# Moving the weight-block additions of a fast-multiplication kernel from VectorE to GpSimd

## The chip, the cores and the metric

One Trainium2 chip, one of its cores. The metric is device time in microseconds (us) of one launch of the whole kernel; the profile is one execution recorded by the hardware profiler. Engines are named as in the profile: PE is TensorE (PEld its weight loads), DVE is VectorE, ACT is ScalarE, POOL is GpSimd, SP is the engine whose queue issues most transfers.

## The reference

One transformer-like block over 528 tokens (16 learned ones ahead of 512) with 1024 features. All big steps are matrix products with large weights:

```
xn = rms_norm(h);  z = xn @ w_in              # 1024 x 10752, cut into 8 parts
o_a = rg_lru(conv(u_rnn)) * gelu(u_gate)      # recurrent branch
o_b = head_rms(retention(q, k, v)) * silu(g_ret)   # 4 heads, decayed attention
mixed = sigmoid(ga) * (o_a @ w_branch_rnn) + sigmoid(gb) * (o_b @ w_branch_ret)
h = h + mixed @ w_out
gate, val = split(conv3(rms_norm(h) @ w_up))  # 1024 x 6144
h = h + (gelu(gate) * val) @ w_down           # 3072 x 1024
out = rms_norm(h)[16:]
```

Inputs and weights are float32.

## The kernel before

Every float32 weight is used as a pair of float16 halves: a high half (scaled by 256 and rounded, a copy on ACT, L92) and a low half (the rest, one SCALAR_TENSOR_TENSOR on DVE, L93, which reads the float32 weight `raw` and the high half `wt`). The helper `split` issues both. A product of two such pairs takes three matmuls (high-high, high-low, low-high).

The weights are cut into *units* of 128 x 2048 numbers. A unit is loaded by SP into one of two `raw` buffers, and split into `wt` tiles of 1024 columns, from a ring of ten. A plain unit fills two `wt` tiles. A *fast* unit is multiplied by a seven-product scheme (Strassen's, in a form that shares sums) in place of eight block products, and fills four tiles: its quarters B11, B21 and B22 as they are, and four sums of quarters, T1 to T4. The steps of a fast unit are

1. `cut(top, left)`: split B11 (512 columns);
2. `cut(low, both)`: split B21 and B22 (1024 columns);
3. `sums`: form T1 to T4 in place in `raw`;
4. two late cuts: `cut(top, both)` splits T1 and T3, `cut(low, both)` splits T4 and T2 (1024 columns each).

There are 39 fast units: 8 for the gate of the retention branch, 4 and 4 for the two mixing gates, 8 for the retention branch's weights, 4 in the up projection and 11 in the down projection. `tick` and `get` emit their steps between the products of earlier units, as far ahead as `ahead[0]` tiles allow. PE, ACT and DVE run in an order written by hand in the first part only; after it a scheduler sets the order, and every engine then takes its instructions strictly in that order. ACT also copies partial products out of PSUM (`kept` and `last`, L872), which PE must have before it reuses the accumulator `pa`; these copies stand in the same queue as the cuts. In the early stages DVE also forms the gates (`g`, L889 to L900) in its one queue with the low halves.

The stages that hold fast units, by their place in the span: value projections and retention with its gates (220 to 400 us), the mixing of the two branches (400 to 650), the output projection without fast units (650 to 714), the up projection (714 to 948) and the down projection (948 to 1050).

Of the kernel before, what the change touches and what calls it, by code (L numbers as in the profile page):

```python
# [12 lines left out]
ALU = mybir.AluOpType  # L13
# [38 lines left out]
def hybrid_block_kernel(ctx, tc, x, meta, norm_mix_g, w_in, conv_w, conv_b, rg_a_w, rg_a_b,  # L52
                        rg_x_w, rg_x_b, lam, w_brnn, w_bret, w_out, norm_ffn_g, w_up,
                        fconv_w, fconv_b, w_down, norm_final_g, rope_t, decay_t, out):
    nc = tc.nc
# [35 lines left out]
    def split(hi, lo, src, s):  # L91
        a = nc.scalar.activation(hi, src, AF.Copy, scale=s)  # L92
        b = nc.vector.scalar_tensor_tensor(lo, src, s, hi, op0=ALU.mult, op1=ALU.subtract)  # L93
        return a.ins, b.ins
# [83 lines left out]
    for ps_ in range(2):  # L178
        for q in range(6):
            rows = w_down[4 * q * P:(4 * q + 4) * P].rearrange("(i j p) c -> p j i c", i=2, j=2)  # L180
# [56 lines left out]
    def fast_steps(rv, bk, bc):  # L237


        tiles = []  # L240
        top, low = slice(0, bk), slice(bk, 2 * bk)
        left, right = slice(0, bc), slice(bc, 2 * bc)

        def cut(rows, cols):
            def run():
                t = wsp.tile([P, 2, 1024], F16, name="wt")
                src = rv[:, rows, cols]
                n = bk * src.shape[2]
                tv = [t[:, a, :n].rearrange("p (k c) -> p k c", k=bk) for a in range(2)]
                tiles.append(tv)  # L250
                split(tv[0], tv[1], src, SW)
            return run

        def sums():
            pair = rv[:, top].rearrange("p k (h c) -> p h k c", h=2)
            nc.vector.tensor_tensor(pair, pair, rv[:, :, right].rearrange("p (h k) c -> p h k c", h=2), op=ALU.add)  # L256
            nc.vector.tensor_tensor(rv[:, low, right], rv[:, top, left], rv[:, low, right], op=ALU.add)
            nc.vector.tensor_tensor(rv[:, low, left], rv[:, low, left], rv[:, low, right], op=ALU.add)  # L258

        at = {"B11": (0, 0), "B21": (1, 0), "B22": (1, bc), "T1": (2, 0), "T3": (2, bc), "T4": (3, 0), "T2": (3, bc)}  # L260

        def form(nm, a, k):
            i, c0 = at[nm]
            return tiles[i][a][:, k, c0:c0 + bc]

        def late(run):
            def behind():
                with behind_copy():
                    run()
            behind.late = True  # L270
            return behind

        wviews.append(form)
        return [cut(top, left), cut(low, slice(0, 2 * bc)), sums,
                late(cut(top, slice(0, 2 * bc))), late(cut(low, slice(0, 2 * bc)))]

# [4 lines left out]
    def behind_copy():  # L281

        return tc.issue_after(last_keep[0]) if gating[0] and last_keep[0] else nullcontext()
# [1392 lines left out]
```

## Time and profile before

| | before |
|---|---|
| time, median of 3 runs | 1069.89 us (1067.33 to 1071.05) |
| span of the profiled execution | 1066.5 us |
| PE busy | 1048.0 us (98%) |
| DVE busy | 853.2 us (80%) |
| ACT busy | 587.9 us (55%) |
| POOL busy | 6.9 us (1%), 20 instructions |

The time of the profiled execution itself is not listed apart; its span is 3.4 us under the median of the three runs. In the views below a group's row gives engine, operation, names, shape, count, then busy time, mean duration of one, and the idle time of the engine just before them with its releaser. In the timeline a row gives start, duration, engine, line and operation, and in brackets the idle time before it. In a table by stretch the columns are stretch, its length, and busy time and count of each engine.

### The profile page before, as it was taken

Reading aid. Unit: us, or ns where it says so; the run is one execution under the profiler, and the core shown is the slowest. Engines: PE = TensorE matmul, PEld = TensorE weight load, DVE = VectorE, ACT = ScalarE, POOL = GpSimd, SP = SyncE. Lnnn points to the kernel's source line nnn. Section 1 sums busy time; section 2 is a strip of 40 time slices with the busy share of each in tenths; the row PEclk is TensorE's granted clock in tenths of the full one; section 3 lists DMA queues with packets and bytes.
Section 4 is the critical chain, followed back from the end, with each engine's and each line's share of the span. In section 5 each row is a group of like instructions: output and inputs, shape, how many; then the busy total and the mean of one; then the engine's idle time right before and its main releaser. Section 6 shows DMA issues by size and latency. Waiting matters only on the chain.

```text
span 1066.5 us, 20995 instructions
## 1 busy us (share of the span) xinstructions
PE 1048.0 (98%) x8995; PEld 851.1 (80%) x8995; DVE 853.2 (80%) x1301; ACT 587.9 (55%) x927; POOL 6.9 (1%) x20
## 2 busy tenths in 40 slices
PE   8999999999999999999999999999999999999997
PEld 6888888865685858887888885588888888888884
DVE  6884799998577878877797776479989897988965
ACT  8568954434364747655554454366566465454442
POOL 2000000000000000000000000000000000000000
PEclk9999999999999999999999999999999999999999
DMA  8341243431022312334433365032432324214322
GB/s 255 104 133 42 80 139 119 160 120 40 2 85 75 120 40 65 119 100 119 129 105 119 115 202 179 1 119 80 159 111 88 119 81 133 67 60 138 101 81 79
DMA packets 108989, 111.49 MB, mean 105 GB/s; under 512 B 5610, under 2 KB 100560, under 8 KB 108896
## 3 DMA queue, kind: packets, MB, share of 16 engines
q1 hardware_dynamic: 108448, 109.74, 32.0%
q8 instruction: 70, 1.15, 0.4%
q10 hardware_dynamic: 160, 0.27, 0.1%
q0 software_dynamic: 288, 0.14, 0.1%
q14 instruction: 23, 0.19, 0.1%
HBM read 108.04 MB, written 2.10 MB: 103 GB/s over the span
## 4 chain that ended last, share of the span: by engine, by line
PE 76%; DVE 13%; ACT 6%; DMA 2%; issue 2%; ACTq 0%; DVEq 0%
PE ps L418 31%; PE P L1512 9%; PE pa L867 7%; PE ps L930 6%; PE ps L1235 4%; DVE wt L93 4%; PE pe L867 3%; PE ps L431 3%; PE pm L418 2%; PE ps L953 2%; PE pa L1399 2%; ACT wt L92 2%; PE pb L867 2%; DVE rnn L665 1%; PE pe L1399 1%
## 5 line engine op out<-in xcount | busy, mean ns | idle before, releaser
L418 PEld LDWEIGHTS <-wt 128*128 128x128 f16 x3840 | 373.2, 97 | 58.2 <-DVE t L759 1.4
L93 DVE SCALAR_TENSOR_TENSOR wt<-raw,wt 128x1024 f16<-128x1024 f32 (+2 forms) x278 | 303.0, 1105 | 58.6 <-ACT wt L92 57.9
L92 ACT ACTIVATE wt<-raw 128x1024 f16<-128x1024 f32 (+2 forms) x278 | 261.4, 962 | 155.7 <-DVE raw L258 30.0
L867 PEld LDWEIGHTS <-wt 128*128 128x128 f16 x2016 | 195.0, 97 | 38.0 <-issue 11.2
L418 PE MATMUL ps<-x2h,wt 128*128 128x258 f16 x1184 | 181.2, 273 | 0.0
L418 PE MATMUL ps<-xh,wt 128*128 128x257 f16 (+2 forms) x1056 | 163.8, 275 | 1.1 <-DVE t L759 1.1
L418 PE MATMUL ps<-x2l,wt 128*128 128x258 f16 x592 | 113.2, 272 | 0.0
L418 PE MATMUL ps<-xl,wt 128*128 128x257 f16 (+2 forms) x528 | 102.2, 275 | 0.0
L1512 PE MATMUL P<-wt,act 128*128 128x256 f16 x792 | 88.3, 273 | 0.0
L1512 PEld LDWEIGHTS <-act 128*128 128x128 f16 x792 | 77.5, 98 | 9.0
L1377 DVE SCALAR_TENSOR_TENSOR cv<-ps,vt,cv 128x512 f32<-128x512 f32 x80 | 59.8, 748 | 22.7 <-ACT cv L1375 21.8
L867 PE MATMUL pa<-xs,wt 128*128 128x257 f16 x576 | 71.6, 273 | 5.1 <-ACT kept L872 4.7
L930 PE MATMUL ps<-wt,xh 128*128 128x512 f16 x256 | 76.1, 379 | 0.4 <-DVE v L93 0.4
L418 PE MATMUL pm<-oa,wt 128*128 128x257 f16 x480 | 55.3, 274 | 0.0
L1375 ACT ACTIVATE cv<-ps,vt,vt 128x512 f32<-128x512 f32 x40 | 30.9, 773 | 34.5 <-PE ps L418 33.8
L930 PE MATMUL ps<-wt,xl 128*128 128x512 f16 x128 | 48.5, 379 | 0.0
L930 PEld LDWEIGHTS <-xh 128*128 128x128 f16 x256 | 24.8, 98 | 29.3 <-issue 0.7
L256 DVE TENSOR_TENSOR raw<-raw 128x1024 f32<-128x1024 f32 x39 | 47.5, 1219 | 0.6
L867 PE MATMUL pa<-ob,wt 128*128 128x257 f16 x384 | 45.7, 274 | 2.0 <-ACT kept L872 1.4
L1235 PE MATMUL ps<-wt,mx 128*128 128x512 f16 x192 | 44.3, 378 | 0.0
L1399 PEld LDWEIGHTS <-wt 128*128 128x128 f16 x336 | 32.6, 97 | 4.4
L1235 PEld LDWEIGHTS <-mx 128*128 128x128 f16 x192 | 17.7, 98 | 18.4
(293 smaller groups left out, 1409.0 us busy)
## 6 DMA issues: line engine op xcount, KB each, us to landing
raw<-in_w_in SPq DMA_DIRECT2D x40, 1024.0 KB, 4.9
raw<-in_w_up SPq DMA_DIRECT2D x24, 1024.0 KB, 5.2
raw<-in_w_down SPq DMA_DIRECT2D x48, 256.0 KB, 3.5
raw<-in_w_branch_ret SPq DMA_DIRECT2D x16, 512.0 KB, 4.7
raw<-in_w_branch_rnn SPq DMA_DIRECT2D x8, 640.0 KB, 4.6
raw<-in_w_out SPq DMA_DIRECT2D x4, 1024.0 KB, 6.2
xin<-in_x SPq DMA_DIRECT2D x4, 512.0 KB, 5.6
raw<-in_w_in SPq DMA_DIRECT2D x4, 512.0 KB, 8.1
```

The costliest lines, as they stand in the source:

```text
L92: a = nc.scalar.activation(hi, src, AF.Copy, scale=s)
L93: b = nc.vector.scalar_tensor_tensor(lo, src, s, hi, op0=ALU.mult, op1=ALU.subtract)
L256: nc.vector.tensor_tensor(pair, pair, rv[:, :, right].rearrange("p (h k) c -> p h k c", h=2), op=ALU.add)
L418: nc.tensor.matmul(ps[:, hf, :n], w(aw, k, col, P), src(ax, k, c0, n), start=k == 0 and (aw, ax) == (0, 0), stop=k == nk - 1 and aw == 1)
L431: mm = nc.tensor.matmul(ps[:, hf, :n], w(aw, k, col, P), src(ax, k, c0, n), start=k == 0 and (aw, ax) == (0, 0), stop=k == KD - 1 and aw == 1)
L867: nc.tensor.matmul(ps[:, :257], ws[k // 4](wf, aw, k % 4), src(xf_, ax, k), start=first and k == 0 and (aw, ax) == (0, 0), stop=k == last_ ...
L930: nc.tensor.matmul(pb, xf(ax, k, XF + j0, nb), w(aw, k % 4, 0, 512), start=i == 0, stop=i == 23)
L1235: nc.tensor.matmul(ps[:, n], mx[k][:, a, c0:c0 + P], wo[k // 2](aw, k % 2, n * 512, 512), start=k == 0 and (a, aw) == (0, 0), stop=k == ks ...
L1375: nc.scalar.activation(vv_, src[:, :, 2:258], AF.Identity, scale=vt2[:, 96 + ch:97 + ch], bias=bias)
L1377: nc.vector.scalar_tensor_tensor(vv_, src[:, :, j:j + 256], vt2[:, 48 * j + ch:48 * j + ch + 1], vv_, op0=ALU.mult, op1=ALU.add)
L1399: nc.tensor.matmul(ps[:, :258], w(wf, aw, k), x2_form(xf_, ax, k), start=first and k == 0 and (aw, ax) == (0, 0), stop=k == 3 and aw == 1, ...
L1512: nc.tensor.matmul(pd[:, 256 * tt:256 * tt + 256], t[:, ax, c0 + tt * P:c0 + tt * P + P], w(wf, aw, i), start=q % 6 == 0 and tt == 0 and i ...
```

## The change

The three DVE additions of `sums` (one of 1024 columns, two of 512) become four additions of 512 columns, issued by GpSimd. The numbers formed are the same. The change is one line longer, so lines below it shift by one: L257 to L259 are the GpSimd additions, L873 is the copy of `kept`.

```
         def sums():
-            pair = rv[:, top].rearrange("p k (h c) -> p h k c", h=2)
-            nc.vector.tensor_tensor(pair, pair, rv[:, :, right].rearrange("p (h k) c -> p h k c", h=2), op=ALU.add)
-            nc.vector.tensor_tensor(rv[:, low, right], rv[:, top, left], rv[:, low, right], op=ALU.add)
-            nc.vector.tensor_tensor(rv[:, low, left], rv[:, low, left], rv[:, low, right], op=ALU.add)
+            for a, rows, cols, b in ((top, top, left, right), (top, low, right, right)):
+                dst = rv[:, a, cols]
+                nc.gpsimd.tensor_tensor(dst, dst, rv[:, rows, b], op=ALU.add)
+            nc.gpsimd.tensor_tensor(rv[:, low, right], rv[:, top, left], rv[:, low, right], op=ALU.add)
+            nc.gpsimd.tensor_tensor(rv[:, low, left], rv[:, low, left], rv[:, low, right], op=ALU.add)
```

The scheduler also puts other instructions in a new order. First place: the queue of DVE in the mixing stage, at the head norm of the last head (`tr`, `rt`, `rc`; about 440 us in the trace). `raw_5367` is the fast unit's weight tile there, `or3` the head's output. Before:

```order
L93 SCALAR_TENSOR_TENSOR wt_5451<-raw_5367,wt_5451 128x512
L976 RECIPROCAL rc_5350<-tr_5348 128x16
L256 TENSOR_TENSOR raw_5367<-raw_5367 128x2x4x128
L978 STREAM_TRANSPOSE rt_5346<-rc_5350 128x512
L93 SCALAR_TENSOR_TENSOR wt_5454<-raw_5367,wt_5454 128x1024
L1043 TENSOR_TENSOR or3_4793<-or3_4793,rt_5346 128x514
L1043 TENSOR_TENSOR or3_4794<-or3_4794,rt_5346 128x514
L257 TENSOR_TENSOR raw_5367<-raw_5367 128x4x128
L93 SCALAR_TENSOR_TENSOR wt_5492<-raw_5367,wt_5492 128x1024
L258 TENSOR_TENSOR raw_5367<-raw_5367 128x4x128
L1043 TENSOR_TENSOR or3_4795<-or3_4795,rt_5346 128x514
```

The same place after the change, where the tile is `raw_5375`:

```order
L93 SCALAR_TENSOR_TENSOR wt_5459<-raw_5375,wt_5459 128x512
L975 STREAM_TRANSPOSE tr_5356<-rt_5354 128x512
L978 RECIPROCAL rt_5354<-rt_5354 128x2
L977 RECIPROCAL rc_5358<-tr_5356 128x16
L93 SCALAR_TENSOR_TENSOR wt_5462<-raw_5375,wt_5462 128x1024
L979 STREAM_TRANSPOSE rt_5354<-rc_5358 128x512
L93 SCALAR_TENSOR_TENSOR wt_5501<-raw_5375,wt_5501 128x1024
L1044 TENSOR_TENSOR or3_4798<-or3_4798,rt_5354 128x514
L1044 TENSOR_TENSOR or3_4799<-or3_4799,rt_5354 128x514
L93 SCALAR_TENSOR_TENSOR wt_5504<-raw_5375,wt_5504 128x1024
L1044 TENSOR_TENSOR or3_4800<-or3_4800,rt_5354 128x514
```

The additions are gone from this queue, and the two late low halves (`wt_5501`, `wt_5504`) stand where DVE must wait for GpSimd's additions, by way of ACT's high halves, with the gating of the head (`or3`) behind them.

Second place: ACT at the same unit, after the change (before, the order is the same here, with `raw_5367`):

```order
L873 ACTIVATE kept_5333<-pa_5337 128x257
L92 ACTIVATE wt_5501<-raw_5375 128x1024
L92 ACTIVATE wt_5504<-raw_5375 128x1024
L92 ACTIVATE wt_5588<-raw_5457 128x640
L92 ACTIVATE wt_5604<-raw_5457 128x640
L873 ACTIVATE last_5334<-pa_5337 128x257
```

The two late high halves, which wait for the additions, stand ahead of the copy `last` that PE needs: nothing moved here, but what they wait for is now another engine.

Third place: the queue of DVE in the down projection, after the change (`raw_11609`, `raw_11714` and `raw_11819` are three units in a row):

```order
L93 SCALAR_TENSOR_TENSOR wt_11765<-raw_11609,wt_11765 128x1024
L93 SCALAR_TENSOR_TENSOR wt_11780<-raw_11609,wt_11780 128x1024
L93 SCALAR_TENSOR_TENSOR wt_11824<-raw_11714,wt_11824 128x512
L93 SCALAR_TENSOR_TENSOR wt_11839<-raw_11714,wt_11839 128x1024
L93 SCALAR_TENSOR_TENSOR wt_11870<-raw_11714,wt_11870 128x1024
L93 SCALAR_TENSOR_TENSOR wt_11885<-raw_11714,wt_11885 128x1024
L93 SCALAR_TENSOR_TENSOR wt_11929<-raw_11819,wt_11929 128x512
```

Before, L256 to L258 stood between these; now one unit's first cut (512 columns) follows the last late cut of the unit before it, so GpSimd cannot start on a unit until that late cut is done.

## The prediction

> **What bounds the kernel now.** I read the page's busy times first (PE 98%), then the table by stretch, the groups of DVE, the waits, and the timeline at two places. The table gives, for each stretch with fast units: length, then busy time of PE, PEld, DVE, ACT and POOL.
>
> ```profile
> 220.00:290.00 70.00, 69.34 (x485) 40.24 (x483) 55.52 (x114) 27.50 (x55) 0.00 (x0) 1.00 0.14 46
> 290.00:400.00 110.00, 109.78 (x884) 77.57 (x883) 83.45 (x132) 64.36 (x107) 0.00 (x0) 1.00 0.23 77
> 400.00:492.00 92.00, 89.01 (x813) 77.35 (x812) 73.95 (x114) 59.41 (x97) 0.00 (x0) 1.00 0.34 102
> 492.00:562.00 70.00, 68.50 (x614) 59.71 (x614) 59.98 (x82) 36.89 (x56) 0.00 (x0) 1.00 0.36 109
> 562.00:650.00 88.00, 85.35 (x760) 73.72 (x758) 66.18 (x87) 43.60 (x65) 0.00 (x0) 1.00 0.46 148
> 714.00:948.00 234.00, 234.00 (x2107) 204.32 (x2106) 205.95 (x304) 132.06 (x193) 0.00 (x0) 1.00 0.32 104
> 948.00:1045.00 97.00, 97.00 (x891) 86.93 (x889) 78.14 (x97) 42.28 (x53) 0.00 (x0) 1.00 0.30 93
> ```
>
> PE is the bound everywhere, at a granted clock of 1.00. It is idle for 0.66 + 0.22 + 2.99 + 1.50 + 2.65 = 8.0 us between 220 and 650, and for nothing from 714 on. So relief of DVE can win 8.0 us at most, and harm has no such limit. The waits say what those 8 us are, and who stands close behind them:
>
> ```profile
> ACT wt L92 <- DVE raw L258: 30.0, 16, 4.2
> ACT wt L92 <- DVE raw L256: 19.5, 16, 3.5
> PEld L867 <- issue: 11.2, 20, 1.7
> PE pa L867 <- ACT kept L872: 6.2, 8, 1.6
> ```
>
> ACT stood 49.5 us, at 32 places, waiting for the additions (L256, L258); PE lost 6.2 us to copies of `kept`, which ACT does in the same queue.
>
> **What is removed.** Rows of DVE by shape:
>
> ```profile
> L93 DVE SCALAR_TENSOR_TENSOR wt<-raw,wt 128x1024 f16<-128x1024 f32 x215 | 260.4, 1219 | 41.0 <-ACT wt L92 40.4
> L256 DVE TENSOR_TENSOR raw<-raw 128x1024 f32<-128x1024 f32 x39 | 47.5, 1219 | 0.6
> L93 DVE SCALAR_TENSOR_TENSOR wt<-raw,wt 128x512 f16<-128x512 f32 x47 | 31.9, 685 | 11.0 <-ACT wt L92 10.9
> L258 DVE TENSOR_TENSOR raw<-raw 128x512 f32<-128x512 f32 x39 | 26.8, 688 | 0.7
> L257 DVE TENSOR_TENSOR raw<-raw 128x512 f32<-128x512 f32 x39 | 26.8, 686 | 0.5
> ```
>
> A unit's additions are 1.219 + 0.686 + 0.688 = 2.59 us, and 39 of them 101.1 us, 12% of DVE's busy time. None of it is on PE itself. What it can win is a share of the 8.0 us: ends 0 and -8.0, none below, since PE has no more idle time there. I take -2, a quarter: only PE's waits for a copy that stands behind a cut can go, and most `kept` gaps are short (6.2 us over 8) and have other causes, such as the copy's own length.
>
> **What is added: the additions' own length.** The trace has no two-input addition on GpSimd. The nearest rows are its fills and its one-input selections:
>
> ```profile
> L348 POOL TENSOR_SCALAR_AFFINE_SELECT same<-same 128x128 f32<-128x128 f32 x2 | 0.8, 396 | 0.0
> L346 POOL MEMSET same<- 128x128 f32 x1 | 0.2, 204 | 0.0
> L1655 POOL MEMSET const-float32-0.0<- 128x1 f32 x1 | 0.1, 104 | 0.3 <-issue 0.3
> ```
>
> A fill costs (204 - 104) / 127 = 0.79 ns per column over a base of 104 ns, so 512 columns 0.51 us; a selection (396 - 104) / 127 = 2.3 ns per column, so 1.28 us. An addition reads two inputs, so it is nearest to the selection, which at least reads one: 1.28 us, with 0.51 as the low end and 2 x 1.28 as the high one. The four of a unit depend on one another through `raw`, and make a chain of 4 x 1.28 = 5.1 us; 156 of them are 200 us of GpSimd's time, which does nothing else after the start (6.9 us in all).
>
> The Trainium skill, page "GPSIMD Engine Reference", section 3.1, gives 4497 ns for such an addition over 2048 columns; scaled to 512 that is an estimate of 1.12 us, a chain of 4.5 us and a sum about 0.6 us x 26 x 0.16 = 2.5 us lower than mine below. No run here shows it yet.
>
> **The chain's length before** was not 2.59 us where DVE was busy. Two units, the slow and the quick end:
>
> ```profile
> 441.01 1.18 DVE L256 TENSOR_TENSOR raw<-raw 128x1024 f32<-128x1024 f32 x1
> 446.78 0.68 DVE L258 TENSOR_TENSOR raw<-raw 128x512 f32<-128x512 f32 x1
> 447.50 1.06 ACT L92 ACTIVATE wt<-raw 128x1024 f16<-128x1024 f32 x1 [4.22 <-DVE raw L258]
> 593.47 1.22 DVE L256 TENSOR_TENSOR raw<-raw 128x1024 f32<-128x1024 f32 x1
> 595.45 0.69 DVE L258 TENSOR_TENSOR raw<-raw 128x512 f32<-128x512 f32 x1
> ```
>
> From the first start to the last end: 6.45 us at 441, because five other DVE instructions stood between, and 2.67 at 593. The middle is 4.56 us. So GpSimd's chain by itself (5.1) is as long as what ACT waits for now: alone it would cost next to nothing.
>
> **The overlap** decides. GpSimd will read the SBUF memory 156 times while DVE does so for the low halves. The trace of before has one such row pair only, and there DVE merely fills a tile:
>
> ```profile
> 1.17 0.27 DVE L493 MEMSET warm<- 128x256 uint32 x1
> 1.19 0.29 POOL masks.py:199 TENSOR_SCALAR_AFFINE_SELECT ident<-ident 128x128 f32<-128x128 f32 x1
> ```
>
> Neither is stretched (0.29 us against 0.396 of the selection above). With two reading engines the ends are: nothing, or taking turns throughout, each new instruction waiting for the whole of the other's. A gain is excluded, since overlap shortens neither. Between ends with no nearer row I take half a turn: an addition waits half a low half, 0.61 us, and a low half half an addition, 0.64.
>
> The Trainium skill speaks against the change here: "SBUF — State Buffer", section "Who interferes with whom", says that a VectorE instruction with two SBUF inputs and a GpSimd one that reads SBUF exclude each other, and that whichever comes second is blocked until the first is through. By that rule, if each meeting cost a whole turn, the sum would be the third rival's +40 us in place of my +10.6. No row of before can show it.
>
> *Mixing stage, by half turns.* The chain becomes 4 x (1.28 + 0.61) = 7.6 us, 3.0 more than 4.56. The ACT waits for additions before the down projection are 32 - 6 = 26, since this view of 948 to 1045 has 3 and 3:
>
> ```profile
> ACT wt L92 <- DVE raw L256: 5.9, 3, 3.5
> ACT wt L92 <- DVE raw L258: 3.3, 3, 2.5
> ```
>
> That is 78 us more of waiting. What PE loses per us of it I take from before: 8.0 us idle to 49.5 us of waiting, 0.16. So +12.6 us. DVE itself: in 492 to 562 it keeps 59.98 - 7 x 2.59 = 41.9 us and gets 28 x 0.64 = 17.9 of blocking, 59.8 of 70, as before: 0. By whole turns 41.9 + 28 x 1.28 = 77.7 of 70, which no longer fits.
>
> *Late loads.* A unit 3 us longer frees its `raw` tile 3 us later and its next load starts so much later. That is part of the same 3 us per unit, not a second one.
>
> *Down projection.* One unit takes PE 9.17 us, from the starts of equal rows:
>
> ```profile
> 957.72 1.47 PE L1512 MATMUL P<-wt,a 128*128 128x256 f16 x12
> 966.89 1.47 PE L1512 MATMUL P<-wt,a 128*128 128x256 f16 x12
> 976.06 1.47 PE L1512 MATMUL P<-wt,a 128*128 128x256 f16 x12
> ```
>
> By the new order a unit's first cut follows the last late cut of the one before, so the cycle is first low half 0.69, four additions 5.1, late high half 1.06, late low half 1.22: 8.1 us, under 9.17. By half turns 8.1 + 4 x 0.61 = 10.5, 1.3 over, 12 us in nine units. The ring of ten tiles is six tiles, or 1.5 units (13.8 us), ahead: 0. By whole turns 8.1 + 4 x 1.22 = 13.0: 9 x 3.8 - 13.8 = +20.
>
> *Up projection.* Four gate units and the first of the down units in 234 us, where PE is never idle and DVE loses 15.6 us of additions: 0, covered by the same ring; if that cover went, at most the 3.0 us per unit.
>
> The sum: -2 + 12.6 + 0 + 0 = +10.6, a span of 1077.1 us. The profiled execution's span lies 3.4 us under the median of the runs, so the time is 1080.5 us. About 0.3% (3.2 us) is what a measurement of this kernel can tell from no change.
>
> **The rivals.**
>
> *No change.* The overlap costs little, and GpSimd's chain of 5.1 us replaces 4.56. The 0.5 us more at 26 places is 13 x 0.16 = +2.1 us, against -2 from relief: 1070.0, with 1067 to 1073. For it: 49.5 us of ACT waiting cost PE only 8.0, and the ring is 1.5 units deep. Against it: low halves fill 260.4 + 31.9 us of DVE, so they must meet the additions often.
>
> *Faster.* At 441, DVE's additions are late because DVE does other work between them; GpSimd would be done at 441.0 + 5.1 = 446.1 instead of 447.46. If an addition takes less than 4.56 / 4 = 1.14 us and overlap is free, ACT waits less everywhere and half or more of the 8.0 us goes: 1062 to 1066. For it: DVE is never free there, as this row of the table by stretch shows (DVE is the third busy time). Against: at places like 593 the chain doubles in length whatever happens.
>
> ```profile
> 441.00:448.00 7.00, 7.00 (x65) 6.13 (x63) 7.00 (x11) 1.85 (x4) 0.00 (x0) 1.00 0.01 2
> ```
>
> *Whole turns.* The chain becomes 4 x (1.28 + 1.22) = 10.0 us: 26 x 5.4 x 0.16 = +22.5, the down projection +20, relief -2: +40, 1110 us.
>
> **How the numbers follow.** Half turns 0.47, no change 0.27, whole turns 0.13, faster 0.13. So faster 0.13, within 0.3% 0.27, slower 0.60. The predicted time is that of half turns, 1080.5; its own range is 1074 (addition at 1.12 or so, turns rare) to 1095 (between half and whole). The range over the cases is 1065 to 1100: it leaves out the better half of the faster case and most of whole turns, under 0.2 together.
>
> **What would show it.** GpSimd rows near 1.28 us each (right) or far off; low halves (L93, 1219 ns now) and the other DVE groups with two SBUF inputs longer than before, while those that read PSUM stay; ACT's wait for `raw` now on POOL, and longer than 49.5 us; PE's idle time between 400 and 650 up by about 10 us, and none after 714. I am wrong if L93 keeps 1219 ns beside running additions, if ACT waits less than 49.5 us, or if PE's loss sits in the up projection.

## The result: 1119.95 us, 4.9% slower

| | median us | runs | ratio to before (95% interval) |
|---|---|---|---|
| before | 1068.66 | 1067.33 to 1071.05, 4 runs | |
| after | 1119.95 | 1119.26 to 1122.13, 4 runs | 1.0488 (1.0467 to 1.0509) |

The sign was forecast, the size was not: +51.3 us in place of +10.6, outside the range. The profiled execution of after spans 1118.2 us, 51.7 more than before. Its page, part 1 (busy time, share of the span, count) and the row of the granted clock:

```profile
PE 1064.1 (95%) x8995; PEld 857.0 (77%) x8995; DVE 832.1 (74%) x1184; ACT 585.3 (52%) x927; POOL 261.2 (23%) x176
PEclk9999999999999999989989999999999999999999
```

The same 8995 matmuls keep PE busy for 16.1 us more (1064.1 against 1048.0), mostly because the granted clock fell in places (mean 0.987, before 0.998); the other 35.6 us of the 51.7 are idle time of PE. DVE lost 117 instructions worth 101 us, and its busy time fell by 21 us only. The groups by shape say why (busy us, mean ns):

```profile
L93 DVE SCALAR_TENSOR_TENSOR wt<-raw,wt 128x1024 f16<-128x1024 f32 x215 | 284.6, 1329 | 109.2 <-ACT wt L92 108.5
L257 POOL TENSOR_TENSOR raw<-raw 128x512 f32<-128x512 f32 x78 | 127.8, 1638 | 787.8 <-DVE wt L93 672.1 <-ACT x2f L92 108.7 <-ACT kept L873 4.0
L259 POOL TENSOR_TENSOR raw<-raw 128x512 f32<-128x512 f32 x39 | 71.6, 1835 | 3.1
L258 POOL TENSOR_TENSOR raw<-raw 128x512 f32<-128x512 f32 x39 | 55.0, 1410 | 33.1 <-DVE wt L93 31.2
L93 DVE SCALAR_TENSOR_TENSOR wt<-raw,wt 128x512 f16<-128x512 f32 x47 | 32.0, 687 | 15.9 <-ACT wt L92 15.9
L986 DVE TENSOR_TENSOR or<-g,or 128x514 f32<-128x514 f32 x16 | 17.3, 1081 | 0.1
```

Both sides are stretched: the low half from 1219 to 1329 ns on average, the gating of `or` from 689 to 1081, and the additions from 1262 ns (the shortest of each of their three lines) to 1410 to 1835. What does not meet an addition (the 512-column halves, 687) keeps its length.

**Where the time went.** The stages end at equal rows: the output projection's first matmul (L1236) stands at 694.27 (649.52 before), the down projection's at 995.13 (948.56). So the stages before the output projection took 44.7 us more, the stretch up to the down projection 1.8, and the rest 5.1. Counted by matmuls, what stands at 400.0 us before stands at 406.9 after, so 6.9 of the 44.7 us fall between 220 and 400. Below, the *mixing stage* is the whole stretch from 220 us to the output projection's first matmul. It carries the result. Its window before, and below it the same 3546 matmuls after (length; busy time of PE, PEld, DVE, ACT, POOL; granted clock):

```profile
220.00:649.52 429.52, 421.49 (x3546) 328.36 (x3544) 338.60 (x526) 231.61 (x376) 0.00 (x0) 1.00 0.30 97
```

```profile
220.00:694.27 474.27, 435.43 (x3546) 334.29 (x3544) 327.94 (x455) 231.22 (x376) 156.25 (x96) 0.97 0.28 88
```

PE's idle time there goes from 8.0 to 38.8 us (+30.8), and its busy time grows by 13.9 at the lower clock: 44.7 together. Who ended PE's idle time, and ACT's waits for the sums, in this window of after:

```profile
ACT wt L92 <- POOL raw L259: 35.4, 16, 4.1
ACT wt L92 <- POOL raw L257: 33.3, 16, 4.5
PEld L868 <- issue: 37.3, 29, 5.5
PE pa L868 <- ACT kept L873: 26.5, 14, 5.3
PE ps L931 <- DVE v L93: 5.4, 3, 2.2
PE pe L868 <- DVE g L894: 2.8, 3, 2.2
```

The copies of `kept` cost PE 26.5 us (6.2 before), and values that DVE itself was late with 8.2 (v and g; 0.4 before). The costliest single place, in the timeline of after (start, length, engine and line; in brackets the idle time before it):

```profile
462.17 1.49 PE L868 MATMUL pa<-xs,wt 128*128 128x257 f16 x12 [1.55 <-ACT last L873]
...
468.40 3.47 POOL L257 TENSOR_TENSOR raw<-raw 128x512 f32<-128x512 f32 x2 [8.91 <-DVE wt L93]
471.95 1.60 POOL L258 TENSOR_TENSOR raw<-raw 128x512 f32<-128x512 f32 x1
473.63 2.12 POOL L259 TENSOR_TENSOR raw<-raw 128x512 f32<-128x512 f32 x1
...
468.52 2.22 DVE L93 SCALAR_TENSOR_TENSOR wt<-raw,wt 128x1024 f16<-128x1024 f32 x1 [0.25 <-ACT wt L92]
470.80 1.63 DVE L986 TENSOR_TENSOR or<-g,or 128x514 f32<-128x514 f32 x1
...
475.79 1.06 ACT L92 ACTIVATE wt<-raw 128x1024 f16<-128x1024 f32 x1 [2.82 <-POOL raw L259]
476.75 0.62 ACT L906 ACTIVATE g<-g 128x514 f32<-128x514 f32 x1
477.27 0.72 ACT L92 ACTIVATE wt<-raw 128x640 f16<-128x640 f32 x1
477.90 0.36 ACT L873 ACTIVATE kept<-pa 128x257 f32<-128x257 f32 x1
...
478.31 2.74 PE L868 MATMUL pa<-xs,wt 128*128 128x257 f16 x12 [5.34 <-ACT kept L873]
```

A low half of 1.22 us takes 2.22 beside an addition. The chain of four takes 7.35 us, from 468.40 to 475.75. ACT waits for its last link, and the copy that PE needs stands behind that cut and two more instructions in ACT's queue. PE idles for 5.34 us. Then the next 12 matmuls take 2.74 us where an equal row (462.17) takes 1.49, and the windows on either side show the clock (the figure behind POOL's count): 0.50 after the gap.

```profile
470.00:478.00 8.00, 2.97 (x25) 2.39 (x24) 5.48 (x5) 4.03 (x8) 5.60 (x3) 0.93 0.00 0
478.00:482.00 4.00, 3.69 (x18) 2.59 (x18) 4.00 (x10) 2.05 (x5) 0.00 (x0) 0.50 0.70 223
```

The Trainium skill, "TensorE: Matmul & The Clock Gate", section "HAM oscillation — how this bites in real kernels", states as a rule that PE should have no idle gap above about 3.4 us, and Part 1 of that page that the clock is then half of the full one. The 0.50 behind this gap agrees. In these runs half the clock also came behind shorter gaps (last section).

### The profile page after: what moved, and what is told of

It reads as the page before. It is cut to its first block, busy times and chain, and to the rows that moved or that the text cites. A ratio compares the mean times of both kernels' runs of the same rounds, so it can differ in the third digit from the quotient of the medians.

```text
span 1118.2 us, 21146 instructions
## 1 busy us (share of the span) xinstructions
PE 1064.1 (95%) x8995; PEld 857.0 (77%) x8995; DVE 832.1 (74%) x1184; ACT 585.3 (52%) x927; POOL 261.2 (23%) x176
## 3 DMA queue, kind: packets, MB, share of 16 engines
q1 hardware_dynamic: 108448, 109.74, 30.8%
## 5 line engine op out<-in xcount | busy, mean ns | idle before, releaser
L93 DVE SCALAR_TENSOR_TENSOR wt<-raw,wt 128x1024 f16<-128x1024 f32 (+2 forms) x278 | 327.8, 1191 | 132.2 <-ACT wt L92 131.3
L419 PEld LDWEIGHTS <-wt 128*128 128x128 f16 x3840 | 374.7, 98 | 61.8 <-DVE cv L1378 1.9
L257 POOL TENSOR_TENSOR raw<-raw 128x512 f32<-128x512 f32 x78 | 127.8, 1638 | 787.8 <-DVE wt L93 672.1
L868 PEld LDWEIGHTS <-wt 128*128 128x128 f16 x2016 | 199.4, 99 | 68.2 <-issue 37.3
L868 PE MATMUL pa<-xs,wt 128*128 128x257 f16 x576 | 76.8, 286 | 27.4 <-ACT kept L873 25.5
L1513 PEld LDWEIGHTS <-act 128*128 128x128 f16 x792 | 77.4, 98 | 13.9 <-issue 3.7
L259 POOL TENSOR_TENSOR raw<-raw 128x512 f32<-128x512 f32 x39 | 71.6, 1835 | 3.1
L258 POOL TENSOR_TENSOR raw<-raw 128x512 f32<-128x512 f32 x39 | 55.0, 1410 | 33.1 <-DVE wt L93 31.2
L419 PE MATMUL pm<-oa,wt 128*128 128x257 f16 x480 | 58.2, 283 | 0.0
L1236 PE MATMUL ps<-wt,mx 128*128 128x512 f16 x192 | 44.3, 379 | 0.0
L1376 ACT ACTIVATE cv<-ps,vt,vt 128x512 f32<-128x512 f32 x40 | 30.8, 769 | 25.6 <-PE ps L419 25.4
```

What stands on the lines that cost most here:

```text
L257: nc.gpsimd.tensor_tensor(dst, dst, rv[:, rows, b], op=ALU.add)
L258: nc.gpsimd.tensor_tensor(rv[:, low, right], rv[:, top, left], rv[:, low, right], op=ALU.add)
L259: nc.gpsimd.tensor_tensor(rv[:, low, left], rv[:, low, left], rv[:, low, right], op=ALU.add)
L419: nc.tensor.matmul(ps[:, hf, :n], w(aw, k, col, P), src(ax, k, c0, n), start=k == 0 and (aw, ax) == (0, 0), stop=k == nk - 1 and aw == 1)
L868: nc.tensor.matmul(ps[:, :257], ws[k // 4](wf, aw, k % 4), src(xf_, ax, k), start=first and k == 0 and (aw, ax) == (0, 0), stop=k == last_ ...
L1236: nc.tensor.matmul(ps[:, n], mx[k][:, a, c0:c0 + P], wo[k // 2](aw, k % 2, n * 512, 512), start=k == 0 and (a, aw) == (0, 0), stop=k == ks ...
```

## The experiments

All times are medians, of eight runs for e1 and e3, three for e8 and two for each of the others. The kernel before ran on the same chip with each group: 1067.48 us for e1 to e4, 1067.46 for e5 to e8, 1067.26 for e9 and e10, 1068.04 for e11. Theory A: GpSimd's reading of SBUF and DVE's instructions with two SBUF inputs take turns. Theory B: the chain of four on one engine, or its place in the order, is too long by itself.

**e1: the chain without reading.** Relative to the changed kernel, `sums` becomes

```
-   four nc.gpsimd.tensor_tensor(...)
+   for n, dst in ((2, rv[:, top, left]), (3, rv[:, top, right]), (2, rv[:, low, right]), (3, rv[:, low, left])):
+       for _ in range(n):
+           nc.gpsimd.memset(dst, 0.5)
```

> The four additions of a unit are replaced by ten GpSimd fills of the same places in the same chain (2, 3, 2 and 3 fills of 512 columns at about 0.51 us, 5.1 us in all), which write SBUF but read nothing; T1 to T4 are not formed. Theory A (turns: a GpSimd instruction that reads SBUF and a DVE instruction with two SBUF inputs hold each other up, and that stretch makes the loss): the chain stays near 5.1 us, the 1024-column low half stays at 1219 to 1225 ns, ACT waits for raw about 50 to 65 us, and the time is 1066 to 1080 us. Theory B (the chain of 5 us is too long by itself, and the copies behind the late cuts in ACT's queue make the loss): low halves also stay at 1219 ns, but the time is 1105 to 1122 us, as with additions.

Measured 1066.05 us, 0.998 (0.9967 to 0.9993) of before. Its groups:

```profile
L93 DVE SCALAR_TENSOR_TENSOR wt<-raw,wt 128x1024 f16<-128x1024 f32 x215 | 261.2, 1220 | 91.2 <-ACT wt L92 90.5
L259 POOL MEMSET raw<- 128x512 f32 x390 | 194.4, 524 | 824.3 <-DMA raw<-in_w_in 313.1 <-DMA raw<-in_w_up 177.5 <-DVE wt L93 162.7
```

With 194 us of GpSimd at work beside it, the low half keeps 1220 ns. DVE is busy for 765.4 us here with the same 1184 instructions as after (832.1), so being blocked cost DVE 66.7 us in after. And the whole relief of DVE is worth 1.4 us, though these fills start earlier than the additions could (see e5): with a chain of about 5 us, more than that was hardly to be won.

**e2 and e3: DVE's sums stay, GpSimd works on `raw` behind the last cut.** e2 adds, e3 fills.

```
+   run()                          # the last late cut of the unit
+   four nc.gpsimd.tensor_tensor on quarters of raw, in place     (e2)
+   ten nc.gpsimd.memset on the same quarters                      (e3)
```

> The additions are made by DVE as in the kernel before, and GpSimd makes four more additions of 512 columns on the unit's raw tile after its last late cut, where nobody waits for them but the next load into that tile. Theory A: the low halves stretch to 1290 to 1340 ns as in the changed kernel, DVE is busy for 30 to 70 us more than 853, and the time is 1078 to 1110 us. Theory B: the time is 1067 to 1073 us, since the chain that ACT waits for is as before.

> As the run before it, with ten GpSimd fills in place of the four further additions, so that the raw tile is given back as late, but nothing is read. Both theories: low halves at 1219 ns. If the late release of the tile is what costs, the time is near that of the run with further additions; theory A has 1067 to 1076 us, theory B the same.

Measured 1174.27 us, 1.0992 (1.0935 to 1.1048), and 1071.67 us, 1.0035 (1.0024 to 1.0047). The fills write the same quarters and read nothing. The late release of `raw` costs 4 us (e3); the additions cost 103 more, above what theory A had expected. Not all of that is DVE's: the reading additions are stretched themselves, so that they hold `raw` for 7.9 us a unit and the fills for 5.7 (means of the first 24 units).

**e4 and e8: one stage at a time.** GpSimd forms the sums of the units before the output projection alone (e4), or of the down projection alone (e8); the other units are summed on DVE as before.

```
+   if u >= u_up[0][0]:     # e8: if u < u_dn[0]:
+       the three additions on nc.vector, as before
+       return
```

> Only the 24 fast units ahead of the output projection have their additions on GpSimd; the 15 units of the up and down projections have them on DVE as before. Both theories put the loss where copies of partial products stand behind the late cuts in ACT's queue: 1105 to 1118 us, PE idle in 400 to 690 about 32 us, a granted clock under 0.95 in places there. If the up and down projections carry more than 15 us of the loss, it is under 1105.

> GpSimd's additions in the units of the down projection alone, the others on VectorE as before. The part of the changed kernel's time that the mixing-only version does not hold: 1119.95 - 1113.92 = 6 us, so 1070 to 1076. In that stage a unit's chain has a period of 10.1 us on GpSimd against 9.17 of PE: 0.9 us x 9 units = 8 us less what the ring of ten tiles covers. If the ring covers all of it, as predicted: 1067 to 1070.

Measured 1113.92 us, 1.0427 (1.0382 to 1.0472), and 1072.36 us, 1.0051 (1.0026 to 1.0075). So +46.4 and +4.9, together the 51.3 of the whole change (the four units of the up projection are on DVE in both). The loss is the mixing stage's, as the milestones say.

**e5: a longer chain without reading.**

```
-   fills (2, 3, 2, 3)
+   fills (3, 4, 3, 4)
```

> As e1_fills, but 14 fills (3, 4, 3, 4) in place of 10, each 0.524 us by e1: a chain of 7.3 us, which is what the four additions took from first start to last end at most places between 430 and 650 in the changed kernel (about 7.0: 436.26 to 443.30, 468.40 to 475.75). The quarters are not summed: T1 to T4 hold a constant. It separates the two ways by which taking turns can cost: the longer chain, or the longer low halves of VectorE. Theory A1, the chain: ACT's wait for raw rises to 110 to 140 us as after, PE is idle for 45 to 55 us, and the time is 1100 to 1120. Theory A2, VectorE's stretched instructions: L93 stays at 1219 ns, and the time is 1064 to 1078 though ACT waits 90 us or more.

Measured 1079.29 us, 1.0112 (1.0083 to 1.0141), near A2's range and far from A1's. But the trace showed a flaw: the first fills went to the quarter that no early cut reads, so the chain began when the load landed or the GpSimd queue came free, 1.3 us or more (4.1 in the middle of 24 units) before the end of the low half that the additions wait for. The same holds for e1 and e10. e9 mends that.

**e6: late cuts held back.**

```
+   hold[0] = 2                                     # at the end of sums
+   if hold[0] > 0 and the next step is a late cut: # in tick
+       hold[0] -= 1
+       return
```

> The changed kernel with the late cuts of a unit held back by two products, so that the copies of kept and last are written ahead of them in ACT's queue. Theory: PE loses because a copy stands behind a late cut that waits for GpSimd: PE's wait for kept falls from 26.5 us to under 12 and the time to 1080 to 1100. Rival: the weights themselves are late (the late products wait for the cuts, whatever stands behind): 1115 to 1135, with PE waiting for wt in place of kept.

Measured 1121.28 us, 1.0505 (1.0475 to 1.0536), with 28.9 us of waiting for `kept`. It decides nothing: most late cuts are issued when a product asks for them, not by `tick`, and ACT's order differed from that of after in one stretch only (416 to 483 us).

**e7: half the additions.** T1 and T3 on GpSimd, T4 and T2 on DVE.

```
-   nc.gpsimd.tensor_tensor(rv[:, low, right], ...); nc.gpsimd.tensor_tensor(rv[:, low, left], ...)
+   nc.vector.tensor_tensor(rv[:, low, right], ...); nc.vector.tensor_tensor(rv[:, low, left], ...)
```

> The first two additions of each unit (T1, T3) on GpSimd, the other two on VectorE, as before: 78 additions in place of 156, of 1.26 us undisturbed. If PE's loss goes with the number of meetings, half of the 51 us: 1090 to 1098. If it goes with what exceeds a slack of ACT's queue (49.5 us of waiting cost 18.5 of PE's idle time, 127.7 cost 54.1): the chain is 2 x 1.6 + 1.4 = 4.6 us, ACT waits 50 to 70 us, and the time is 1068 to 1080.

Measured 1091.51 us, 1.0226 (1.0183 to 1.0270): +24.0 for 78 additions, +51.3 for 156. Half the additions cost half the loss. In the mixing stage ACT waited for the sums for 10.5 us more than before (47.2 against 36.7, table below), against 32.0 more in after, and PE's idle time still grew by 18.6. So the loss goes with the additions more than with that wait; one point doesn't show a law.

**e9: the chain's length alone, matched.** Eight fills of 1024 columns, one behind the other; the first waits for the first low half, like the additions.

```
+   for dst in (rv[:, top],) * 4 + (rv[:, low],) * 4:
+       with (tc.issue_after(f.ins) if f else nullcontext()):
+           f = nc.gpsimd.memset(dst, 0.5)
```

> A fill chain that starts where the additions start: four fills of the upper 1024 columns, which wait for the first low half like the additions do (in e5 the fill of the quarter that no early cut reads went first, 1.4 us sooner), then four of the lower 1024, one behind the other. A 1024-column fill is estimated at 104 + 1024 x 0.82 = 0.94 us from e1's 524 ns for 512, so the chain is 7.5 us, as the additions' (7.45 us on average over 24 units before the output projection). The sums are not formed. If the length of the chain alone makes PE late: output projection at 690 or later, 1105 to 1120 us. If the stretched instructions of VectorE are needed too: L93 stays at 1219 ns, the output projection starts at 655 to 672, and the time is 1078 to 1095.

Measured 1098.57 us, 1.0286 (1.0249 to 1.0324), a little above the second range. Its low halves, and its mixing stage with the waits there:

```profile
L93 DVE SCALAR_TENSOR_TENSOR wt<-raw,wt 128x1024 f16<-128x1024 f32 x215 | 261.1, 1221 | 147.6 <-ACT wt L92 147.0
```

```profile
220.00:669.58 449.58, 425.87 (x3545) 328.19 (x3543) 282.66 (x452) 228.29 (x375) 181.50 (x192) 1.00 0.29 90
```

```profile
ACT wt L92 <- POOL raw L260: 85.8, 37, 4.6
PE pa L869 <- ACT kept L874: 10.9, 12, 2.3
PE pa L869 <- ACT last L874: 8.7, 6, 2.3
```

A chain of 7.90 us, even somewhat longer than the additions' 7.45 (the mean of 24 units of after), costs the mixing stage 20.1 us, at a granted clock of 1.00 and with no gap of PE above 2.31 us. ACT waits longer here than in after (85.8 us against 68.7), and PE loses half as much. So the chain's length explains about 20 of the 44.7 us, and theory B falls as the whole cause. Two things make the 20 a size and no strict bound: 4 of the 24 chains of after are longer than 7.91 us (up to 9.96), and the scheduler's order of the instructions is not the same in the two kernels. Behind the start of the down projection e9 loses 9.6 us, more than after's 5.1.

**e10: one input.** Four `nc.gpsimd.tensor_scalar(q, q, 1.0, None, op0=ALU.mult)` on the four quarters.

> The four additions of a unit replaced by four GpSimd multiplications by 1.0 in place on the same quarters, which read one SBUF input in place of two (the sums are not formed). If reading SBUF at all makes GpSimd and VectorE take turns: L93 1300 ns or more, instructions above 1.2 us often, and 1095 to 1115. If it takes GpSimd's second input: GpSimd rows all near one length, L93 at 1219, and 1064 to 1072.

Measured 1096.64 us, 1.0268 (1.0233 to 1.0304), in the first range.

```profile
L93 DVE SCALAR_TENSOR_TENSOR wt<-raw,wt 128x1024 f16<-128x1024 f32 x215 | 267.4, 1249 | 120.9 <-ACT wt L92 119.8
L258 POOL TENSOR_SCALAR raw<-raw 128x512 f32<-128x512 f32 x156 | 259.6, 1677 | 792.8 <-DMA raw<-in_w_in 267.9 <-DVE wt L93 152.4 <-DVE g L893 104.6
```

A multiplication takes 1479 to 1492 ns where nothing meets it (the shortest and the median), and up to 2932. One input is enough for turns, but DVE is blocked for 18.6 us (784.0 busy against e1's 765.4), not 66.7. The expected 1300 ns of L93 was too much. The early start helps this kernel as it helps e5, whose fills read nothing and cost 11.8 us in all; the multiplications cost 29.4.

**e11: turns without a chain.** DVE forms the sums; GpSimd adds on a scratch tile that nothing waits for.

```
+   nc.gpsimd.tensor_tensor(shade[:, 0:1], shade[:, 0:1], rv[:, 2 * bk - 1, 0:1], op=ALU.mult)
+   for _ in range(4):
+       nc.gpsimd.tensor_tensor(shade, shade, shade, op=ALU.add)
    the three additions on nc.vector, as before
```

> VectorE forms the sums as in the kernel before, and nothing waits for GpSimd: it makes four additions of 512 columns per unit on a scratch tile of its own, in place, started when the unit's load has landed (by a one-column product that reads the last row block of raw and that the third sum waits for; one of 46 pieces gives the space). The order of the other engines is that of before. This is the taking of turns alone, without the longer chain of the sums that e9 priced at 31 us and without the late release of raw in e2. If turns cost only by the chain on GpSimd: 1064 to 1075. If they also cost by making VectorE's own work late, as 1119.95 - 1098.57 = 21 us would say: 1080 to 1100, L93 above 1300 ns, PE waiting for v and g of VectorE (9.7 us in the changed kernel, 0.9 before); up to 1130 if VectorE's sums are stretched like its low halves.

Measured 1135.42 us, 1.0629 (1.0598 to 1.0660): +67.4 us, above even the 1130 given for stretched sums, though the sums don't pass through GpSimd. Its groups and its mixing stage:

```profile
L261 POOL TENSOR_TENSOR shade<-shade 128x512 f32<-128x512 f32 x156 | 226.8, 1454 | 12.2
L263 DVE TENSOR_TENSOR raw<-raw 128x1024 f32<-128x1024 f32 x39 | 57.7, 1480 | 0.6
```

```profile
220.00:704.67 484.67, 438.88 (x3544) 334.48 (x3542) 401.38 (x527) 231.06 (x376) 148.91 (x118) 0.96 0.27 86
```

DVE's 1301 instructions are those of before and take 100.7 us longer (953.9 against 853.2). Its own sums are stretched too (1480 ns for 1219), and ACT waits longer for them (73.8 us), so this is more than the turns cost in after. That they cost without any wait for GpSimd is shown: no engine's idle time ends with a GpSimd addition or with the one-column product here. Nor is it a matter of a new order: PE and ACT take their instructions in the order of before, and DVE too, but for one low half of `mx`.

The mixing stage of these kernels side by side, from windows that end at the output projection's first matmul and from the waits in them:

| kernel | length us | PE busy | PE idle | ACT's wait for the sums | clock |
|---|---|---|---|---|---|
| before | 429.5 | 421.5 | 8.0 | 36.7 | 1.00 |
| e1, short fills | 427.1 | 421.2 | 5.9 | 23.5 | 1.00 |
| e5, early fills | 433.5 | 421.7 | 11.8 | 32.7 | 1.00 |
| e10, multiplications | 449.1 | 427.2 | 21.9 | 50.4 | 0.99 |
| e9, matched fills | 449.6 | 425.9 | 23.7 | 85.8 | 1.00 |
| e7, two additions | 454.1 | 427.5 | 26.6 | 47.2 | 0.99 |
| after | 474.3 | 435.4 | 38.8 | 68.7 | 0.97 |
| e11, private additions | 484.7 | 438.9 | 45.8 | 73.8 | 0.96 |
| e2, additions behind | 513.7 | 445.4 | 68.3 | 64.6 | 0.94 |

## Why the prediction missed

**Right.** An undisturbed addition takes 1262 ns; the selection's slope gave 1.28 us, and the estimate of 1.12 from the Trainium skill's "GPSIMD Engine Reference", section 3.1, was low. The chain in the mixing stage came to 7.45 us on average against 7.6. That closeness is in part luck: an addition was held up by 0.37 us on average and DVE by 0.43 per addition, where half turns had 0.61 and 0.64, and 0.94 us of the chain are gaps between its additions, which the sum did not have. The relief was worth 1.4 us (e1) against 2. Turns fall on instructions with two SBUF inputs against a GpSimd instruction that reads: fills leave L93 at 1220 ns; in after, the 57 low halves of 1024 columns that ran beside an addition took 1630 ns on average and the other 158 took 1220. A DVE addition with one input from PSUM (`g`, L901) took 416 ns at 11 places beside an addition and 420 at 9 others. That is the rule of the Trainium skill, "SBUF — State Buffer", section "Who interferes with whom", which also says that GpSimd's writing alone is free of it; e1, e3 and e9 agree with that too. PE lost in the mixing stage, as said.

**The step that failed is the price of the mixing stage:** 78 us of ACT's waiting at 0.16 = +12.6, measured +44.7.

- *The amount.* ACT's wait rose by 78.2 us over the whole kernel (68.0 + 59.7 - 49.5), and that it is my 78 is chance. In the mixing stage it rose by 32.0 (36.7 at 24 places to 68.7 at 32); the other 46.2 lie behind it, where PE lost 1.8 + 5.1.
- *The ratio.* 0.16 was an average over waiting that before hid nearly all of. The added 32.0 us went with 30.8 us of PE's idle time, 0.96 each. Even that is no price to carry over: in the table, e9 waits longest of all, and of the last six rows only e10 idles less. Waiting of an engine that is not the bound was the wrong quantity; what counts is whether the one copy or value that PE needs next stands behind it.
- *"DVE itself: 0."* I compared DVE's load with the length of the stretch and found room. But an engine with room is late all the same when each piece of a dependent sequence is stretched. PE waited 9.9 us for values straight from DVE in the mixing stage (v 5.4, g 2.8, two kinds of sf 0.9 and 0.6, ssum 0.2), 0.9 before, and e11 lost 55.2 us there with no engine waiting for GpSimd.
- *The clock.* It was not in the sum at all: PE's busy time grew by 13.9 us in the mixing stage, a third of its loss. The clock was at half there in 8 steps of 3.41 us, which is 13.7 us of lost work. Gaps of some 2 us and more make it (last section), so it comes on top of the idle time only once gaps grow.

So of the 44.7 us, a chain as long as e9's takes about 20.1; the other 24.6 or so need the turns. Against e9, 15.1 of these are idle time of PE (28.5 us of waiting for copies against 19.6, 9.9 for DVE's values against 0.8, none for weights against 2.9) and 9.5 are busy time. The runs don't separate them further, since DVE's lateness also lengthens the copies' gaps.

*Down projection: 0, covered.* Measured +4.9 (e8). The cycle was 10.1 us against PE's 9.17 (the second of the L257 additions starts at 1020.12, 1030.22 and 1040.33), close to the 10.5 of half turns. The ring did cover that excess: in after PE waited 0.2 us for weights there. What it lost came by DVE's queue again, at one place:

```profile
1052.07 1.06 ACT L92 ACTIVATE wt<-raw 128x1024 f16<-128x1024 f32 x1 [3.88 <-POOL raw L257]
1053.16 1.30 DVE L93 SCALAR_TENSOR_TENSOR wt<-raw,wt 128x1024 f16<-128x1024 f32 x1 [1.65 <-ACT wt L92]
1054.39 0.68 DVE L1539 TENSOR_TENSOR s<-P,s 128x512 f32<-128x512 f32 x1
1055.12 1.47 PE L1513 MATMUL P<-wt,act 128*128 128x256 f16 x12 [2.08 <-DVE s L1539]
```

DVE's addition `s`, which reads the accumulator `P` that PE needs next, stands behind a low half that waits, by way of ACT, for GpSimd. PE idles for 2.08 us there and for 1.58 us at the next three such places. The sum had priced only late weights. In e9, with a cycle of 10.9 us, the ring did run out: PE waited 6.2 us for weights.

*Up projection: 0*: measured +1.8; PE waited 1.7 us for one value of DVE (`cv`). *From span to median: 3.4*: in after 1.75 (1119.95 against 1118.2).

Of the rivals, whole turns came nearest in time (1110) with the wrong mechanism: its mean chain of 10.0 us was not there (7.45), and the down projection, which was to give half of its loss, gave a tenth.

## What to carry to other kernels

Work moved from VectorE to GpSimd is not beside VectorE's if both read SBUF, VectorE with two inputs: price the blocking of both, and follow it to the value that the bounding engine needs next, in the order of the queue in which that value is made. Never price a new wait by the average loss per waited microsecond of a schedule that hides its waits. Before costing such a move, replace the moved work by something that only writes: if it starts no later than the moved work would, one run tells about how much the relief can be worth, here 1.4 us.

## What the runs showed of the hardware

- A GpSimd multiplication of one input by a constant, 512 columns of float32, takes 1.49 us, longer than the addition of two inputs (1.26); a fill takes 0.524 us for 512 columns and 0.952 for 1024.
- The clock after a gap of PE, by the length of the next 12 equal matmuls (1.49 us at full clock): 2.74 us behind gaps of 5.34, 4.70 and 3.94 us; 2.46 behind 3.20 and 2.05 behind 3.45; but 1.49 behind 2.87, and 2.72 behind one of 2.41. So the length of one gap alone does not decide between 2.4 and 3.5 us. The first two 2.74, the 2.46 and the 2.72 are after's, the others e10's.
- What decides in these traces is a fixed grid in time. In the ten traces with half clock behind 200 us (after, e2 and e4 to e11), all its stretches start on one grid of 3.413 us per trace (in after at 467.0, 477.2, 497.7, 572.8, 630.8 and 664.9 in the mixing stage) and, but for the one at each kernel's end, last one, two or three steps. Leaving out each kernel's last 12 us, all 50 steps at full clock in which PE idled for 1.99 us or more were followed by a step at half, and none with 1.98 or less. So e10's gap of 2.87 us, 1.6 of it on one side of a step's edge and 1.2 on the other, cost nothing, and after's 2.41, all in one step, did.
- Busy time of PE in e9's mixing stage rose by 4.4 us. One step at half clock (544.8 to 548.2) explains 1.7 of it. What the rest is stays open; matmul ends are modelled in the trace.
